# Low parts of weights and left multiplies of an attention stage on VectorE instead of GpSimd

## The chip, the cores and the metric

The kernel runs on one core of one Trainium2 chip. The core has TensorE (PE) for matmuls and transposes, VectorE (DVE) and ScalarE (ACT) for elementwise work, GpSimd (POOL) for elementwise work on SBUF, and SyncE (SP), which issues DMAs. The metric is the device time of one execution in microseconds, the median of several runs.

## The reference

One layer of a hybrid encoder: 1024 tokens, 1024 channels, float32. A normalised input is projected once; the parts feed a convolution branch and an attention branch, which are gated, merged and projected; then comes a SwiGLU block. The attention is a stick-breaking one with 8 heads of 64 channels. What is computed of a block of 128 queries:

```python
z = jnp.einsum('bqhd,bkhd->bhqk', qb, kb) * scale
log_1m = jnp.where(mask, jax.nn.log_sigmoid(-z), 0.0)
rev_excl = lax.cumsum(log_1m, axis=3, reverse=True) - log_1m
a = jnp.where(mask, jnp.exp(jax.nn.log_sigmoid(z) + rev_excl), 0.0)
outs.append(jnp.einsum('bhqk,bkhd->bqhd', a, vb))
```

So a weight is sigmoid(z) times the product of sigmoid(-z) over all later allowed keys.

## The kernel before

**Precision.** Matmul operands are kept as a high part and a low part; the low part is the operand less its high part. `load_w` (L64) does this for weights: a DMA of 128 x 1024 into `wraw`, an ACT copy into `wh` (L70), a subtraction into `wl` (L71). L71 runs on the engine given by `sub`, else on GpSimd. `mm3` and `dense_T` (L74 to L91) multiply with them; `wl` is read in the last third of a product (L80). Without an argument the tiles `wraw`, `wh` and `wl` have two buffers each.

**First stage, up to about 50 us.** Eight blocks of 128 tokens are fetched (`xt`), squared on ACT with the sum kept (`junk`, L172), scaled: DVE adds epsilon (`pv`, L101), GpSimd takes the power -1/2 (`pr`, L105), DVE multiplies (`xt`, L175). TensorE transposes (`tp`, L113), ACT and DVE make high and low parts (`hH` L115, `hL` L116), and a product for the values of heads 0 to 3 follows (`psv`, L137 to L139; `vt`, L142 and L143). The two weights of that product have `sub=V` already.

**Attention stage, about 50 to 352 us.** For each head and each pair of query blocks (m = 0 to 3), `chunk` makes a row of up to 512 keys: two matmuls into `z`, a mask on the diagonal (DVE, L246), sigmoid(-z) into one of two tiles `qf` (ACT, L251), sigmoid(z) into `sg` (L252). DVE then runs the product from right to left along the row (`R`: L255 for the chunk with the diagonal, L260 for the chunk left of it, which starts from the first one's last value) and multiplies by `sg` (L257, or L261 for the left chunk). L261 runs on GpSimd: 128 x 512, 32 times, only for m = 2 and 3 and thus for four rows of a head. GpSimd also writes a column of zeros into `R` (L256) and zeros into the unused quarter of `aH` and `aL` (L324). TensorE transposes the rows (`tpa`, L315), ACT and DVE split them (`aH` L320, `aL` L321), and TensorE multiplies with the values (`av`, L290 and L291), of which there is one PSUM buffer; ACT and DVE empty it (`avt` L296, `ar` L299).

**Work laid between.** A table (`at`) gives the projections of later heads and of the convolution branch to steps of this loop: `psk`, `psq`, `psv`, `psg`, each a product of 24 matmuls of 512 columns (or of 256 for `psv`). Fifteen weights are loaded for them from the first stage on: eight for keys and queries, two for values, five for the other branch.

**Order.** A scheduler sets the order on each engine from the program's order, its buffers and its own costs of the instructions; each engine then runs its list strictly in order.

Of the kernel before, what the change touches and what calls it, by code (L numbers as in the profile page):

```python
# [7 lines left out]
F32 = mybir.dt.float32  # L8
# [3 lines left out]
ALU = mybir.AluOpType  # L12
# [25 lines left out]
def layer_kernel(ctx, tc, x, vecs, dww, gains, ident_d, mask_d, wv, wi, wbr, wo, wu, wdq, wd, out):  # L38
    nc = tc.nc
    PE, V, A, G, SP = nc.tensor, nc.vector, nc.scalar, nc.gpsimd, nc.sync  # L40

    def pool(name, bufs=1, **kw):
        return tc.tile_pool(name=name, bufs=bufs, reuse_waits="tile", **kw)
# [17 lines left out]
    hH = big.tile([P, NK, S], F32R, name="hH")  # L61
    hL = big.tile([P, NK, S], F32R, name="hL")

    def load_w(src, pl=None, bufs=2, n=1024, sub=None):  # L64
        pl = pl or wst
        raw = wst.tile([P, 1024], F32, name="wraw", tag="wraw", bufs=2)[:, 0:n]
        SP.dma_start(out=raw, in_=src)
        wh = pl.tile([P, n], F32R, name="wh", tag="wh", bufs=bufs)
        wl = pl.tile([P, n], F32R, name="wl", tag="wl", bufs=bufs)
        A.activation(out=wh, in_=raw, func=AF.Copy)  # L70
        (sub or G).tensor_tensor(out=wl, in0=raw, in1=wh.bitcast(F32), op=ALU.subtract)  # L71
        return wh, wl

    def mm3(ps, steps, first=True, last=True):  # L74
# [72 lines left out]
    with pool("prep") as pp:  # L147
# [31 lines left out]
        fetch(1)  # L179
        transpose_split(psz, "z", xts[0], 0)  # L180
        wvt.append(load_w(wv[0, 0], pp, sub=V))
        pre(1)
        wvt.append(load_w(wv[0, 1], pp, sub=V))
        for tb in range(1, NT):
            if tb + 1 < NT:
# [49 lines left out]
    def chunk(par, qk, i, c, n, diag, carry):  # L235
        ks, (qhs, ql) = qk
        kst, qh = ks[par], qhs[par]
        r = slice(par * 64, par * 64 + 64)
        ts_ = slice(i * P, (i + 1) * P)
        nn = max(n, 256)  # L240
        z = psz.tile([P, HALF], F32, name="z", tag="z")
        cs = slice(c * HALF, c * HALF + nn)
        PE.matmul(z[:, 0:nn], lhsT=qh[:, ts_], rhs=kst[:, cs], start=True, stop=False)
        PE.matmul(z[:, 0:nn], lhsT=ql[par][:, ts_], rhs=kst[:, cs], start=False, stop=True)
        if diag:
            V.tensor_tensor(out=z[:, n - P:n], in0=z[:, n - P:n], in1=mask, op=ALU.add)  # L246
        sg = ap_.tile([P, HALF], F32, name="sg", tag="sg", bufs=3)
        q = qfix[qturn[0] % len(qfix)]
        qturn[0] += 1
        R = ap_.tile([P, HALF + 8], F32, name="R", tag="R", bufs=RBUFS)  # L250
        A.activation(out=q[:, 0:n], in_=z[:, 0:n], func=AF.Sigmoid, scale=-1.0)  # L251
        A.activation(out=sg[:, 0:n], in_=z[:, 0:n], func=AF.Sigmoid)  # L252
        if diag:
            d = q[:, 0:n][:, ::-1]
            V.tensor_tensor_scan(out=R[:, 3:3 + n][:, ::-1], data0=d, data1=d, initial=1.0, op0=ALU.mult, op1=ALU.bypass)  # L255
            G.memset(R[:, 3 + n:4 + n], 0.0)  # L256
            V.tensor_tensor(out=R[:, 4:3 + n], in0=sg[:, 0:n - 1], in1=R[:, 4:3 + n], op=ALU.mult)  # L257
        else:
            d = q[:, 1:n + 1][:, ::-1]
            V.tensor_tensor_scan(out=R[:, 4:4 + n][:, ::-1], data0=d, data1=d, initial=carry, op0=ALU.mult, op1=ALU.bypass)  # L260
            G.tensor_tensor(out=R[:, 4:4 + n], in0=sg[:, 0:n], in1=R[:, 4:4 + n], op=ALU.mult)  # L261
        return R

    def rows_of(h, m, qk):
        rows = []
        for ii in range(2):
            i = 2 * m + ii
            n_all = (i + 1) * P
            if n_all > HALF:
                r1 = chunk(h % 2, qk, i, 1, n_all - HALF, True, None)  # L270
                r0 = chunk(h % 2, qk, i, 0, HALF, False, r1[:, 3:4])
                rows.append((r0, r1))
            else:
                rows.append((chunk(h % 2, qk, i, 0, n_all, True, None), None))
        return rows
# [61 lines left out]
    def load_pair(pr, what):  # L337
        wts[what] = load_w(wi[(12 if what == "k" else 8) + pr])
        if what == "k":
            pairs[pr] = ([ap_.tile([P, S], F32R, name="kst", tag=f"k{j}", bufs=1 + j) for j in range(2)], None)  # L340
        else:
            qh = [ap_.tile([P, S], F32R, name="qh", tag=f"q{j}", bufs=1 + j) for j in range(2)]
            ql = [ap_.tile([P, S], F32R, name="ql", tag=f"ql{j}", bufs=1 + j) for j in range(2)]
            for j in range(2):
                G.memset(ql[j][64 - j * 64:128 - j * 64, :].bitcast(F32), 0.0)
            pairs[pr] = (pairs[pr][0], (qh, ql))
# [82 lines left out]
    def bank(nm):  # L429
        return ps8.tile([P, HALF], F32, name=nm, tag="d")  # L430

    with pool("mix") as mp:
        ones = mp.tile([P, P], F32, name="ones")
        avg = mp.tile([P, P], F32, name="avg")
# [641 lines left out]
    PE, V, A, G, SP = [Ordered(e) for e in (PE, V, A, G, SP)]  # L1076
# [152 lines left out]
```

## Time and profile before

| | |
|---|---|
| median of 3 runs (lowest, highest) | 1464.91 us (1461.34, 1465.78) |
| profiled execution | 1465.04 us |
| its span in the trace | 1463.2 us |
| busy: PE, DVE, ACT, POOL | 1374.1, 1057.3, 528.6, 282.3 us |
| low parts of weights on POOL (L71), whole program | 58 times, 141.0 us |
| left multiplies on POOL (L261) | 32 times, 46.7 us |

Busy time is that in which an engine executes an instruction; idle time ahead of an instruction is put down to what ended last before it. TensorE's busy time is modelled, since its instructions overlap. The granted clock is given as a share of 2.4 GHz. The chain of waits goes back from the last instruction: at each step to what released it, or to the one before it on its engine.

### The profile page before, as it was taken

The page shows a single profiled execution, that of the slowest core. Times are in us where ns is not written, and L with a number is a line of the kernel's source. Part 1 is how long each engine was busy: PE and PEld are TensorE (multiplying, and loading weights), DVE is VectorE, ACT ScalarE, POOL GpSimd, SP SyncE. Part 2 cuts the span into 40 slices and gives each one's busy share as a digit, 9 for nine tenths or more (in the row PEclk, how much of TensorE's full clock was granted, in tenths as well). Part 3 has the DMA queues.
Part 4 walks back from the last instruction along what each step waited for, and adds up shares of the span by engine and source line. Part 5 has one row for each costly group of instructions (what it writes and reads, how often), then busy time and mean ns, then how long its engine had stood idle before and what let it go on. Part 6 is the DMA issues. An engine that isn't in the chain of part 4 may idle for free.

```text
span 1463.2 us, 17209 instructions
## 1 busy us (share of the span) xinstructions
PE 1374.1 (94%) x6412; PEld 1126.8 (77%) x6412; DVE 1057.3 (72%) x1385; ACT 528.6 (36%) x863; POOL 282.3 (19%) x301
## 2 busy tenths in 40 slices
PE   6988998998999979999999799999999998999987
PEld 6866787777888757887787588888888887888875
DVE  5498878776999996325348899888877785644564
ACT  5466656553111104323325223222222222633450
POOL 2134323332324232322306200000000000000130
PEclk9999999999999989999999899999999999999999
DMA  6001001101111110212522155444444445965273
GB/s 221 23 26 40 22 23 32 42 30 36 45 49 52 43 44 22 65 43 81 172 87 94 65 198 184 174 157 158 143 149 162 166 137 178 371 230 177 89 272 100
DMA packets 62403, 160.97 MB, mean 110 GB/s; under 512 B 6384, under 2 KB 17904, under 8 KB 62320
## 3 DMA queue, kind: packets, MB, share of 16 engines
q1 hardware_dynamic: 62032, 158.83, 32.2%
q8 instruction: 50, 0.82, 0.2%
q10 hardware_dynamic: 288, 1.05, 0.2%
q14 instruction: 33, 0.27, 0.1%
HBM read 117.65 MB, written 40.11 MB: 108 GB/s over the span
## 4 chain that ended last, share of the span: by engine, by line
PE 66%; DVE 22%; issue 5%; ACT 3%; DMA 2%; POOL 2%; SPq 0%; DVEq 0%; POOLq 0%; ACTq 0%
PE m L914 28%; PE md L914 12%; DVE acc L453 11%; PE pg L77 2%; PE pg L78 2%; PE pg L80 2%; DVE R L260 2%; DVE R L255 2%; PE po L670 1%; PE po L669 1%; PE po L668 1%; DVE aL L321 1%; DVE R L257 1%; PE av L291 1%; PE pb L78 1%
## 5 line engine op out<-in xcount | busy, mean ns | idle before, releaser
L71 POOL TENSOR_TENSOR wl<-wraw,wh 128x1024 fp32r<-128x1024 f32 (+1 forms) x58 | 141.0, 2438 | 248.7 <-ACT wh L70 145.7
L453 DVE SCALAR_TENSOR_TENSOR acc<-u,dw,acc 128x1024 f32<-128x1024 f32 x120 | 176.9, 1531 | 0.3
L914 PE MATMUL m<-t,wh 128*128 128x512 f32 x528 | 134.8, 397 | 4.4 <-ACT wh L914 3.0
L914 PE MATMUL m<-hH,wh 128*128 128x512 f32 x328 | 130.6, 398 | 8.8 <-ACT wh L776 8.8
L914 PE MATMUL md<-wl,wh 128*128 128x512 f32 x308 | 122.5, 398 | 9.5 <-DVE wl L914 9.5
L914 PE MATMUL m<-hL,wh 128*128 128x512 f32 x328 | 129.9, 396 | 0.0
L914 PEld LDWEIGHTS m<-t,wh 128*128 128x128 f32 x528 | 100.0, 190 | 29.0 <-ACT wh L914 3.4
L914 PE MATMUL md<-wh 128*128 128x512 f32 x308 | 122.0, 396 | 0.0
L914 ACT ACTIVATE c<-c 128x512 f32<-128x512 f32 x44 | 27.8, 633 | 244.4 <-DVE c L914 244.4
L914 POOL TENSOR_TENSOR dc<-dc,gpo 128x512 f32<-128x512 f32 x4 | 5.1, 1301 | 541.4 <-ACT junk L914 541.4
L70 ACT ACTIVATE wh<-wraw 128x1024 fp32r<-128x1024 f32 (+1 forms) x60 | 56.5, 945 | 144.4 <-PE pg L78 50.7
L77 PE MATMUL pg<-hH,wh 128*128 128x512 f32 x256 | 101.5, 396 | 0.0
L78 PE MATMUL pg<-hL,wh 128*128 128x512 f32 x256 | 100.0, 391 | 0.0
L914 PE MATMUL md<-wh,wl 128*128 128x512 f32 x308 | 98.8, 395 | 0.0
L914 PE MATMUL m<-hH,wl 128*128 128x512 f32 x328 | 89.2, 393 | 0.0
L914 PEld LDWEIGHTS m<-hH,wh 128*128 128x128 f32 x328 | 62.2, 190 | 23.7 <-ACT wh L776 9.2
L914 PEld LDWEIGHTS md<-wl,wh 128*128 128x128 f32 x308 | 58.9, 191 | 24.5 <-DVE wl L914 11.8
L914 DVE TENSOR_TENSOR wl<-ra,wh 128x1024 fp32r<-128x1024 f32 (+1 forms) x42 | 48.4, 1153 | 38.1 <-ACT wh L914 38.0
L914 PEld LDWEIGHTS m<-hL,wh 128*128 128x128 f32 x328 | 62.2, 190 | 14.1
L914 PEld LDWEIGHTS m<-hH,wl 128*128 128x128 f32 x328 | 61.6, 188 | 14.3
L914 PE MATMUL m<-t,wl 128*128 128x512 f32 x264 | 70.7, 390 | 0.0
L914 DVE TENSOR_TENSOR u<-m,u 128x512 f32<-128x512 f32 x66 | 45.4, 688 | 33.5 <-PE m L914 32.1
(226 smaller groups left out, 3303.2 us busy)
## 6 DMA issues: line engine op xcount, KB each, us to landing
ra<-act SPq DMA_DIRECT2D x35, 512.0 KB, 6.8
wraw<-in_wi SPq DMA_DIRECT2D x32, 512.0 KB, 3.5
rg<-in_wu SPq DMA_DIRECT2D x23, 512.0 KB, 4.4
ru<-in_wu SPq DMA_DIRECT2D x22, 512.0 KB, 5.3
q<-in_wdq SPq DMA_DIRECT2D x22, 512.0 KB, 6.1
wsum<-q SPq DMA_DIRECT2D x22, 512.0 KB, 2.6
act<-sa SPq DMA_DIRECT2D x44, 256.0 KB, 2.7
rb<-wsum SPq DMA_DIRECT2D x20, 512.0 KB, 8.7
```

What stands on the lines that cost most here:

```text
L70: A.activation(out=wh, in_=raw, func=AF.Copy)
L71: (sub or G).tensor_tensor(out=wl, in0=raw, in1=wh.bitcast(F32), op=ALU.subtract)
L77: PE.matmul(ps, lhsT=lh, rhs=rh, start=(first and j == 0), stop=False)
L78: PE.matmul(ps, lhsT=lh, rhs=rl, start=False, stop=False)
L80: PE.matmul(ps, lhsT=ll, rhs=rh, start=False, stop=(last and j == n - 1))
L255: V.tensor_tensor_scan(out=R[:, 3:3 + n][:, ::-1], data0=d, data1=d, initial=1.0, op0=ALU.mult, op1=ALU.bypass)
L257: V.tensor_tensor(out=R[:, 4:3 + n], in0=sg[:, 0:n - 1], in1=R[:, 4:3 + n], op=ALU.mult)
L260: V.tensor_tensor_scan(out=R[:, 4:4 + n][:, ::-1], data0=d, data1=d, initial=carry, op0=ALU.mult, op1=ALU.bypass)
L291: PE.matmul(av, lhsT=vt[j][:, hh, :], rhs=aL[:, jj, :], start=False, stop=(j == 2 * m + 1))
L321: V.tensor_tensor(out=flat[1][:, 0:n * P], in0=tpf, in1=flat[0][:, 0:n * P].bitcast(F32), op=ALU.subtract)
L453: V.scalar_tensor_tensor(out=acc, in0=u[:, kk:kk + S], scalar=dw[:, cb, kk:kk + 1], in1=acc, op0=ALU.mult, op1=ALU.add)
L914: return lambda *a, **k: tc.keep_in_program_order(fn(*a, **k))
```

## The change

A variable holds the engine of L71 where no `sub` is given: VectorE up to the end of the attention stage, GpSimd after it. The multiply of the left chunk becomes a VectorE instruction.

```diff
+    low_of = [V]
...
-        (sub or G).tensor_tensor(out=wl, in0=raw, in1=wh.bitcast(F32), op=ALU.subtract)
+        (sub or low_of[0]).tensor_tensor(out=wl, in0=raw, in1=wh.bitcast(F32), op=ALU.subtract)
...
-            G.tensor_tensor(out=R[:, 4:4 + n], in0=sg[:, 0:n], in1=R[:, 4:4 + n], op=ALU.mult)
+            V.tensor_tensor(out=R[:, 4:4 + n], in0=sg[:, 0:n], in1=R[:, 4:4 + n], op=ALU.mult)
...
+    low_of[0] = G
     with pool("mix") as mp:
```

15 subtractions and 32 multiplies pass from GpSimd's list to VectorE's; no instruction is added or removed. Lines after the first insertion are numbered 2 higher in the kernel after (L71 is L73, L261 is L263), and the scheduler sets a new order on every engine within the first 352 us.

GpSimd in the first stage, before (`pr` is the power of a block, `wl` a low part):

```order
L105 TENSOR_TENSOR pr_213<-pv_211,mhalf_77 128x1
L71 TENSOR_TENSOR wl_554<-wraw_551,wh_553 128x1024
L105 TENSOR_TENSOR pr_265<-pv_263,mhalf_77 128x1
L71 TENSOR_TENSOR wl_562<-wraw_559,wh_561 128x1024
L105 TENSOR_TENSOR pr_317<-pv_315,mhalf_77 128x1
```

After, the same place on VectorE, where the two low parts now stand (`xt_258` is the block that `pr_265` scales):

```order
L103 TENSOR_SCALAR pv_263<-sst_261 128x1
L73 TENSOR_TENSOR wl_554<-wraw_551,wh_553 128x1024
L145 TENSOR_TENSOR vt_255<-psv_230,vt_255 128x4x64
L177 SCALAR_TENSOR_TENSOR xt_258<-xt_258,pr_265,gpre_101 128x1024
L118 TENSOR_TENSOR hL_79<-tp_268,hH_78 128x4x128
L118 TENSOR_TENSOR hL_79<-tp_275,hH_78 128x4x128
L145 TENSOR_TENSOR vt_307<-psv_282,vt_307 128x4x64
L103 TENSOR_SCALAR pv_315<-sst_313 128x1
L73 TENSOR_TENSOR wl_562<-wraw_559,wh_561 128x1024
```

The powers follow each other on GpSimd with nothing between, and a low part stands ahead of the scaling on VectorE.

VectorE in head 2 for m = 2 and 3, before (rows of the table `R` by number; L260 is the product of a left chunk, L257 the multiply of a diagonal chunk):

```order
L260 SCALAR_TENSOR_TENSOR R_1436<-qf1_549,R_1426 128x512
L255 SCALAR_TENSOR_TENSOR R_1446<-qf0_547 128x256
L246 TENSOR_TENSOR z_1497<-z_1497,mask_74 128x128
L257 TENSOR_TENSOR R_1446<-sg_1445,R_1446 128x255
L260 SCALAR_TENSOR_TENSOR R_1456<-qf1_549,R_1446 128x512
L255 SCALAR_TENSOR_TENSOR R_1502<-qf0_547 128x384
```

After:

```order
L262 SCALAR_TENSOR_TENSOR R_1436<-qf1_549,R_1426 128x512
L257 SCALAR_TENSOR_TENSOR R_1446<-qf0_547 128x256
L263 TENSOR_TENSOR R_1436<-sg_1435,R_1436 128x512
L259 TENSOR_TENSOR R_1446<-sg_1445,R_1446 128x255
L262 SCALAR_TENSOR_TENSOR R_1456<-qf1_549,R_1446 128x512
L323 TENSOR_TENSOR aL_1488<-tpa_1483,aH_1487 128x384
L263 TENSOR_TENSOR R_1456<-sg_1455,R_1456 128x512
```

The left multiply (L263) stands one or two instructions behind its product.

TensorE in the same phase, m = 3, before (`psk` is a projection of later heads):

```order
L243 MATMUL z<-kst,qh 128x512
L244 MATMUL z<-kst,ql 128x512
L291 MATMUL av<-aL,vt 128x256
L77 MATMUL psk<-hH,wh 128x512
L315 MATMUL tpa<-ident,R 128x128 x2
L78 MATMUL psk<-hL,wh 128x512
L243 MATMUL z<-kst,qh 128x512
```

After:

```order
L245 MATMUL z<-kst,qh 128x512
L246 MATMUL z<-kst,ql 128x512
L80 MATMUL psk<-hL,wh 128x512
L79 MATMUL psk<-hH,wh 128x512
L80 MATMUL psk<-hL,wh 128x512
L79 MATMUL psk<-hH,wh 128x512
L80 MATMUL psk<-hL,wh 128x512
L79 MATMUL psk<-hH,wh 128x512
L80 MATMUL psk<-hL,wh 128x512
L82 MATMUL psk<-hH,wl 128x512
L317 MATMUL tpa<-ident,R 128x128
L245 MATMUL z<-kst,qh 128x512
```

More of the projection stands ahead of the transposes of the left chunks. Counted up to the last `z` of a head, 3, 15, 14, 9 and 10 more matmuls of projections have been issued in heads 0, 1, 2, 3 and 5 than before; at the next query pair or two the counts are level again.

## Rows read from the trace of the kernel before

**Rows 1.** Chain of waits, 20 to 352 us: shares of the stretch by engine and line.
```profile
by line: DVE R L260 8.1%; issue 6.9%; DVE R L255 6.9%; DVE aL L321 5.3%; DVE R L257 4.5%; PE av L291 4.4%; PE tpa L315 4.2%; PE av L290 3.9%; PE psg L80 3.8%; PE psv L137 3.5%; PE psv L139 3.5%; PE psv L138 3.5%; PE psg L78 3.4%; PE psg L77
```

**Rows 2.** Windows of the attention stage: from:to and length, then the columns named.
```profile
core 0: us, PE busy (x) PEld busy (x) DVE busy (x) ACT busy (x) POOL busy (x), PEclk, DMA share, GB/s
20.00:352.00 332.00, 303.08 (x1786) 256.48 (x1786) 249.77 (x408) 185.56 (x377) 110.51 (x196) 0.99 0.13 37
20.00:40.00 20.00, 17.41 (x138) 17.11 (x138) 15.21 (x23) 13.02 (x25) 7.60 (x9) 0.91 0.51 159
76.00:121.00 45.00, 36.57 (x205) 28.52 (x204) 43.20 (x70) 29.11 (x64) 16.86 (x32) 1.00 0.08 21
121.00:139.00 18.00, 17.86 (x105) 14.50 (x103) 13.56 (x28) 11.44 (x24) 5.91 (x12) 1.00 0.24 63
139.00:152.00 13.00, 8.18 (x43) 6.17 (x42) 13.00 (x17) 7.95 (x18) 7.18 (x7) 1.00 0.05 17
152.00:170.00 18.00, 18.00 (x98) 15.75 (x97) 14.25 (x29) 10.28 (x22) 1.83 (x13) 0.91 0.06 15
245.00:261.00 16.00, 12.58 (x65) 9.72 (x64) 14.19 (x19) 8.53 (x17) 6.05 (x8) 1.00 0.07 17
261.00:280.00 19.00, 18.87 (x104) 15.52 (x104) 14.09 (x29) 11.51 (x24) 5.94 (x13) 1.00 0.19 51
```

**Rows 3.** Groups by line and shape, 20 to 352 us: busy us, mean ns | idle, releasers.
```profile
L71 POOL TENSOR_TENSOR wl<-wraw,wh 128x1024 fp32r<-128x1024 f32 x16 | 39.5, 2470 | 70.9 <-ACT wh L70 67.8 <-ACT sg L252 3.0
L261 POOL TENSOR_TENSOR R<-sg,R 128x512 f32<-128x512 f32 x32 | 46.7, 1461 | 81.1 <-DVE R L260 77.6 <-PE tpa L315 1.8 <-ACT aH L320 1.6
L257 DVE TENSOR_TENSOR R<-sg,R 128x511 f32<-128x511 f32 x16 | 14.9, 933 | 0.6
L257 DVE TENSOR_TENSOR R<-sg,R 128x255 f32<-128x255 f32 x16 | 13.4, 840 | 0.9
L255 DVE TENSOR_TENSOR_SCAN R<-qf 128x512 f32<-128x512 f32 x16 | 21.7, 1358 | 2.6 <-ACT qf L251 2.0 <-PE tpa L315 0.5
L175 DVE SCALAR_TENSOR_TENSOR xt<-xt,pr,gpre 128x1024 f32<-128x1024 f32 x5 | 8.5, 1703 | 3.8 <-POOL pr L105 3.8
```

**Rows 4.** Timeline of VectorE, two heads: start us, length us, instruction, count.
```profile
148.34 1.53 DVE L257 TENSOR_TENSOR R<-sg,R 128x511 f32<-128x511 f32 x1
...
152.23 1.20 DVE L321 TENSOR_TENSOR aL<-tpa,aH 128x512 fp32r<-128x512 f32 x2
...
157.02 0.41 DVE L257 TENSOR_TENSOR R<-sg,R 128x255 f32<-128x255 f32 x1
...
161.98 1.22 DVE L255 TENSOR_TENSOR_SCAN R<-qf 128x512 f32<-128x512 f32 x1
163.31 0.69 DVE L257 TENSOR_TENSOR R<-sg,R 128x511 f32<-128x511 f32 x1
```

**Rows 5.** Timeline of GpSimd beside the first row of group 4.
```profile
147.26 2.07 POOL L261 TENSOR_TENSOR R<-sg,R 128x512 f32<-128x512 f32 x1 [0.58 <-DVE R L260]
```

**Rows 6.** Timeline of VectorE while the input is normalised.
```profile
12.66 1.22 DVE L71 TENSOR_TENSOR wl<-wraw,wh 128x1024 fp32r<-128x1024 f32 x1
...
21.59 1.28 DVE L175 SCALAR_TENSOR_TENSOR xt<-xt,pr,gpre 128x1024 f32<-128x1024 f32 x1 [0.66 <-POOL pr L105]
...
23.99 0.14 DVE L101 TENSOR_SCALAR pv<-sst 128x1 f32<-128x1 f32 x1
...
26.38 3.38 DVE L175 SCALAR_TENSOR_TENSOR xt<-xt,pr,gpre 128x1024 f32<-128x1024 f32 x1 [0.99 <-POOL pr L105]
```

**Rows 7.** Timeline of GpSimd in the same stretch.
```profile
23.45 2.40 POOL L71 TENSOR_TENSOR wl<-wraw,wh 128x1024 fp32r<-128x1024 f32 x1 [1.90 <-ACT wh L70]
25.80 0.55 POOL L105 TENSOR_TENSOR pr<-pv,mhalf 128x1 f32<-128x1 f32 x1
```

**Rows 8.** Timeline of TensorE: transposes of the input, and eight matmuls of a projection.
```profile
29.91 1.94 PE L113 MATMUL tp<-ident,xt 128*128 128x128 f32 x8 [2.59 <-DVE xt L175]
...
58.23 1.98 PE L80 MATMUL psq<-hH,wl 128*128 128x512 f32 x8
```

## The prediction

> **What bounds the kernel now.** Everything that the change touches ends before 352 us, so I read that part alone. First the chain of waits [rows 1]: its longest single entries are VectorE's products, multiplies and low parts (L260, L255, L321, L257: 24.8% of the stretch), and the rest is TensorE's lines, each of 3 to 4%. GpSimd stands nowhere among them. So two engines take turns as the bound. The windows say where [rows 2]. Over 20 to 352 us TensorE is busy 303.1 us of 332 and VectorE 249.8; what TensorE can still gain here is its 28.9 us of idle time. From 139 to 152 us VectorE is busy all 13.0 us and TensorE 8.2: this is head 2 at m = 2 and 3, where the left chunks are. 76 to 121 us (heads 0 and 1: 43.2 us of 45) and 245 to 261 us (head 5: 14.2 of 16) look alike. Between them, at 121 to 139, 152 to 170 and 261 to 280 us, projections run, TensorE is full and VectorE has 4.4, 3.8 and 4.9 us free.
>
> Then the two engines beside each other. A multiply of 511 columns on VectorE took 0.69 us at 163.31, with GpSimd doing nothing, and 1.53 us at 148.34 [rows 4], while GpSimd's left multiply ran from 147.26 to 149.33, 2.07 us against a mean of 1.46 [rows 3, 5]. The two do not overlap; they wait for each other. The part of VectorE's busy time that is really such waiting is the key to this change.
>
> **The change part by part.** The sum is made against the profiled execution, 1465.04 us, which lies 0.13 us above the median of the three runs; its span is 1463.2 us, and the 1.8 us around it stay.
>
> *What VectorE gets.* A left multiply has 512 columns, as the low part `aL` at 152.23 us, of which two took 1.20 us [rows 4]: 0.60 us each in a row of work, 0.69 alone. 32 x 0.60 = 19.2 us. A low part of a weight took VectorE 1.22 us [rows 6], of which about 0.08 lies under the next instruction: 15 x 1.14 = 17.1 us. Together 36.3 us.
>
> *What VectorE no longer waits for.* From the means of groups 3 less the lengths alone: 255 columns (0.84 - 0.41) x 16 = 6.9; 511 columns (0.93 - 0.69) x 16 = 3.9; products of 512 columns (1.36 - 1.22) x 16 = 2.2; scaling of the input (1.70 - 1.28) x 5 = 2.1 [rows 3, 4, 6]. Together 15.1 us, and the net load is +21.2 us. Where it falls decides.
>
> *The saturated stretches* hold the left multiplies of heads 0, 1, 2 and 5. At 139 to 152 us three multiplies were delayed as the one in group 4, by 0.84 us each: 2.5 us given back against 4 x 0.60 = 2.4 added, net nothing. On the mean over the eight heads 10.8 / 8 = 1.35 us is given back (from the 255 and 511 columns), net +1.05 us per head. Four heads: between 0 and +4.2 us; I take +2.0.
>
> *The first stage.* GpSimd made a low part from 23.45 to 25.85 us, and the power of the next block, asked for by `pv` at 24.0, came only at 25.80 [rows 6, 7]. The scaling of that block then took 3.38 us instead of 1.28, and TensorE sat 2.59 us before its transposes at 29.91 [rows 6, 8]. The clock granted from 20 to 40 us is 0.91, between the two levels of 1.2 and 2.4 GHz, which is 1.8 us lost; the fall comes with this gap, and the eight transposes after it took 1.94 us. Without the low part on GpSimd the power is ready near 24.7. VectorE has the low part (1.14) and a `vt` ahead of the scaling, which then ends near 27.0 instead of 29.8, when TensorE runs out of earlier work at 27.3 (29.91 less 2.59). So the gap goes, and most of the lost clock: -2.6 - 1.4 = -4.0 us; between -1.5 (another wait takes half the gap, the clock still falls) and -4.4. TensorE has work from here to 76 us, so what is gained here stays.
>
> *The order on TensorE.* 15, 14 and 10 projection matmuls are issued earlier, inside the saturated phases of heads 1, 2 and 5, where TensorE is idle. One takes 0.25 us (eight in 1.98 [rows 8]): 3.7, 3.5 and 2.5 us, which the full stretches behind would lose. They can lose only what VectorE has free there, less two low parts of 1.14 in the first and the last: 2.1, 3.8 and 2.6 us [rows 2]. The smaller of each pair: 2.1 + 3.5 + 2.5 = 8.1 us at most. At least 0: TensorE also takes its list strictly in order, and a projection that stands before a `z` can hold back VectorE's next row. I take half, -4.0 us.
>
> *Elsewhere* (other weights, heads 3, 4, 6, 7) TensorE is the bound and VectorE's free time covers the load; I take 0. If the cover is gone it costs: the heads have 16 left multiplies at most, net 4 x 1.05 = 4.2 us, and a low part on the path 1.14 us. GpSimd is left with small fills, so the zeros that TensorE sometimes waits for come no later.
>
> Sum: 1465.0 - 4.0 + 2.0 - 4.0 = **1459 us**.
>
> **The rivals.** *The new order gives nothing (1463 us).* VectorE, 21 us heavier, needs all of its free time, and the projections moved forward only change which gap TensorE has: -4.0 + 2.0 alone. For it speaks that the full stretches had 13.1 us free on VectorE and four low parts and later splits go there; against it, that the moved matmuls lie exactly in the saturated phases.
>
> *VectorE becomes the bound (1472 us, slower).* Its list is strictly in order, and a low part waits for ACT's `wh`. On GpSimd this wait was long, 67.8 us over the stage [rows 3], and cost nothing, since only small fills stood behind. On VectorE the products, multiplies and splits of the next row stand behind, and for those ACT, TensorE's transposes and the one `av` buffer wait. If half of the net load ends on the path: -4.0 + 10.6 = +6.6; all of it would be 1482. It decides as soon as the low parts stand ahead of their `wh`, or VectorE's free time in a projection stretch is less than the two low parts put there (2.3 us of 4.4 at 121 to 139 us). The Trainium skill, "Perfetto Trace Analysis", section "Optimizing Scalar/DVE Operations", speaks for this rival: with a saturated VectorE it may make sense to give work away, to GpSimd too, and this change does the reverse. The same section adds that the two share a read port of SBUF, so that moving between them might not help; the rows of group 4 and 5 agree with that second half, 1.53 us against 0.69.
>
> *All idle time in the saturated phases is used (1452 us).* The moved matmuls give all 8.1 us, and the saturated heads cost 0 instead of 2, with a little off TensorE's waits for the left rows: 1465.0 - 4.4 - 8.1 = 1452.5. For it: GpSimd's multiply ended some 1.3 to 2 us behind its product, VectorE's 0.7.
>
> That the change doesn't do what it says is excluded by the order: 47 instructions stand on the other engine.
>
> **How the numbers follow.** A measurement of this kernel can tell about 0.3%, 4.4 us, from no change. Forecast 1459 (itself 1455 to 1462): 0.42, of which 0.34 lies more than 4.4 us below the time before. New order gives nothing: 0.26, no change. VectorE the bound: 0.22, of which 0.18 is slower by more than 4.4 us. All idle time used: 0.10. Faster 0.34 + 0.10 = 0.44; slower 0.18; within 0.3% 0.38. The range reaches from 1450, the last rival with a little more off the first stage's waits, to 1470, the first part of the slower one.
>
> **What would show it.** Right: the multiplies of 255 and 511 columns at 0.41 and 0.69 us throughout; a left multiply of 0.69 us on VectorE; no gap of 2.6 us on TensorE near 30 us and a granted clock near 1.0 there; the conv stage starting about 6 us earlier than 352 us with its own length unchanged; VectorE still full in head 2, TensorE's idle time of 28.9 us down by some 6. Wrong: idle time on VectorE in front of low parts, ended by ACT's `wh`; TensorE's waits for `ar` and `aL` grown; the first stage ending as late as before; or a loss of clock in a place that had none.

## The result, and the profile after

| | before | after |
|---|---|---|
| median (lowest to highest, runs) | 1464.64 us (1461.34 to 1465.78, 4) | 1452.53 us (1452.17 to 1453.70, 4) |
| ratio, 95% interval | | 0.9922 (0.9905 to 0.9940) |
| profiled execution's span | 1463.2 us | 1450.4 us |

The changed kernel is faster by 0.8%, 12.1 us by the medians. By the traces 10.8 of 12.8 us lie in the attention stage: its end (the first low part of the attention outputs) moves from 353.1 to 342.3 us, and what follows takes nearly as long as before (1110.1 us before, 1108.1 after). The line numbers after are those of before plus 2 (plus 3 behind the attention stage).

The same windows as in [rows 2], for the changed kernel. The first is the stage; the others are the ramp, heads 0 and 1, the stretch behind them, head 2 at m = 2 and 3, the stretch behind it, and head 5:

```profile
core 0: us, PE busy (x) PEld busy (x) DVE busy (x) ACT busy (x) POOL busy (x), PEclk, DMA share, GB/s
20.00:341.00 321.00, 302.97 (x1777) 252.75 (x1775) 266.08 (x453) 183.12 (x376) 31.39 (x149) 0.99 0.13 38
20.00:40.00 20.00, 19.57 (x168) 19.23 (x166) 17.37 (x28) 13.95 (x27) 6.33 (x11) 1.00 0.51 164
72.00:116.00 44.00, 39.41 (x213) 30.45 (x213) 42.47 (x74) 29.00 (x63) 4.30 (x23) 1.00 0.05 16
116.00:133.00 17.00, 16.44 (x102) 13.42 (x100) 16.64 (x33) 11.89 (x27) 1.35 (x11) 1.00 0.17 48
133.00:147.00 14.00, 12.28 (x57) 8.34 (x55) 13.56 (x22) 7.36 (x15) 1.36 (x4) 1.00 0.14 39
147.00:163.00 16.00, 15.71 (x90) 12.83 (x91) 15.46 (x31) 10.86 (x25) 1.37 (x11) 1.00 0.07 16
236.00:252.00 16.00, 13.59 (x60) 10.44 (x59) 15.25 (x23) 9.22 (x17) 0.59 (x5) 0.89 0.07 17
```

TensorE is as busy as before (303.0 us against 303.1), in 321 us instead of 332: its idle time fell from 28.9 to 18.0 us, and that is the gain. VectorE's busy time rose from 249.8 to 266.1 us. In the saturated places TensorE's idle time fell from 8.4 us of 45 to 4.6 of 44 (heads 0 and 1), from 4.8 of 13 to 1.7 of 14 (head 2), from 3.4 of 16 to 2.4 of 16 (head 5). VectorE is still full in head 2, 13.6 us of 14, and these places are about as long as before: what changed is that TensorE does more in them.

What TensorE waited for in the stage; each row gives the waiting line, the releaser, us in total, times and the longest. First the kernel before:

```profile
PE av L290 <- DVE ar L299: 7.8, 5, 1.8
PE tpa L315 <- DVE aL L321: 7.4, 4, 2.2
PE av L291 <- DVE aL L321: 3.5, 6, 1.4
PE tpa L315 <- POOL R L256: 3.1, 2, 1.7
PE tpa L315 <- POOL R L261: 2.7, 2, 1.4
PE tp L113 <- DVE xt L175: 2.6, 1, 2.6
```

Then the changed kernel:

```profile
PE tpa L317 <- DVE aL L323: 5.1, 5, 1.9
PE av L293 <- DVE aL L323: 5.0, 8, 1.3
PE av L292 <- DVE ar L301: 2.2, 3, 1.2
PE tpa L317 <- DVE R L259: 1.4, 3, 0.6
PE tpa L317 <- DVE R L263: 1.3, 3, 0.6
```

The waits for GpSimd's `R` (3.1 + 2.7 us, one line being its multiply, the other a fill queued behind it) are gone, and 2.7 us of waits for VectorE's `R` took their place. The waits for `ar` fell from 7.8 to 2.2 us, the one for `xt` from 2.6 to 0.4. Those for `aL` stayed: 10.9 before, 10.1 after. Together -11.7 us, against -10.9 us of idle time: smaller waits grew by 0.8 us, above all those of `z` for ACT's `sg`, from 0.2 to 1.2.

The groups by line and shape on VectorE (busy us, mean ns, then idle time just before and its releasers), which answer to [rows 3]:

```profile
L263 DVE TENSOR_TENSOR R<-sg,R 128x512 f32<-128x512 f32 x32 | 21.7, 680 | 1.2 <-DVE R L262 0.5
L257 DVE TENSOR_TENSOR_SCAN R<-qf 128x512 f32<-128x512 f32 x16 | 19.4, 1213 | 0.7 <-ACT qf L253 0.7
L73 DVE TENSOR_TENSOR wl<-wraw,wh 128x1024 fp32r<-128x1024 f32 x15 | 18.3, 1217 | 8.4 <-PE psg L82 5.8 <-ACT wh L72 1.7 <-PE psq L82 0.8
...
L259 DVE TENSOR_TENSOR R<-sg,R 128x511 f32<-128x511 f32 x16 | 10.9, 682 | 0.4
...
L259 DVE TENSOR_TENSOR R<-sg,R 128x255 f32<-128x255 f32 x16 | 6.7, 420 | 0.2
L177 DVE SCALAR_TENSOR_TENSOR xt<-xt,pr,gpre 128x1024 f32<-128x1024 f32 x5 | 6.4, 1283 | 1.2 <-POOL pr L107 1.1
```

Every form now has the length that it had alone. The 255 columns went from 840 to 420 ns on the mean, the 511 from 933 to 682, the scaling of the input from 1703 to 1283. For what follows I call **hold-up** the net time by which VectorE's instructions with a GpSimd instruction of over 0.25 us beside them are longer than the median of the same form and line without one, summed over the attention stage from 20 us on (some are a little shorter and count against it). It is 17.7 us in the kernel before and 0.0 after; 22 instructions are clearly longer, by over 0.05 us each, and these are counted in brackets below.

### The profile page after: what moved, and what is told of

It reads as the page before. It is cut to its first block, busy times and chain, and to the rows that moved or that the text cites. A ratio compares the mean times of both kernels' runs of the same rounds, so it can differ in the third digit from the quotient of the medians.

```text
span 1450.4 us, 17204 instructions
## 1 busy us (share of the span) xinstructions
PE 1371.0 (95%) x6412; PEld 1120.5 (77%) x6412; DVE 1073.4 (74%) x1432; ACT 527.8 (36%) x863; POOL 203.6 (14%) x254
## 4 chain that ended last, share of the span: by engine, by line
PE 64%; DVE 23%; issue 5%; ACT 3%; POOL 2%; DMA 2%; SPq 0%; DVEq 0%; POOLq 0%; ACTq 0%
PE m L917 28%; PE md L917 12%; DVE acc L456 11%; PE pg L79 2%; PE pg L82 2%; PE pg L80 2%; DVE R L262 2%; DVE R L257 2%; PE po L673 1%; PE po L672 1%; DVE aL L323 1%; PE po L671 1%; DVE R L259 1%; PE tpa L317 1%; PE psg L82 1%
## 5 line engine op out<-in xcount | busy, mean ns | idle before, releaser
L456 DVE SCALAR_TENSOR_TENSOR acc<-u,dw,acc 128x1024 f32<-128x1024 f32 x120 | 177.0, 1534 | 0.3
L73 POOL TENSOR_TENSOR wl<-wraw,wh 128x1024 fp32r<-128x1024 f32 (+1 forms) x43 | 104.3, 2434 | 192.2 <-PE pg L82 96.7
```

Of the source, the lines that this page charges most:

```text
L73: (sub or low_of[0]).tensor_tensor(out=wl, in0=raw, in1=wh.bitcast(F32), op=ALU.subtract)
L456: V.scalar_tensor_tensor(out=acc, in0=u[:, kk:kk + S], scalar=dw[:, cb, kk:kk + 1], in1=acc, op0=ALU.mult, op1=ALU.add)
```

## The experiments

Two theories stood against each other. The prediction's own: separate gains (a shorter first stage, projections moved ahead on TensorE) against a heavier VectorE; they should add up. The other: while any two-input work stays on GpSimd, it and VectorE hold each other up, and what counts is that both kinds of work leave. In the first four expectations the prediction's account is theory 1 and the hold-ups are theory 2; in the later ones the hold-ups are theory 1. The kernels were timed in four groups, each beside the kernel before, whose median was 1464.6, 1464.9, 1465.3 and 1466.0 us in them. "us" is (ratio - 1) x 1465, and a difference of two such numbers is uncertain by about 2 to 3 us. Differences between kernels are given by the ratios, with that of the medians in brackets.

| kernel | median us | ratio (95% interval) | us | hold-up us (instructions) |
|---|---|---|---|---|
| changed kernel | 1452.53 | 0.9922 (0.9905 to 0.9940) | -11.4 | 0.0 |
| low parts alone moved | 1460.98 | 0.9972 (0.9961 to 0.9983) | -4.1 | 10.0 (14) |
| multiplies alone moved | 1468.41 | 1.0021 (1.0012 to 1.0030) | +3.1 | 12.8 (10) |
| first two low parts alone | 1462.44 | 0.9986 (0.9978 to 0.9995) | -2.1 | 15.6 (21) |
| all but the first two low parts | 1456.21 | 0.9939 (0.9927 to 0.9951) | -8.9 | 2.0 (1) |
| spare work on GpSimd, free to run ahead | 1472.95 | 1.0050 (1.0035 to 1.0064) | +7.3 | 2.0 (8) |
| spare work on VectorE, free to run ahead | 1457.32 | 0.9944 (0.9929 to 0.9960) | -8.2 | 0.0 |
| left multiplies of heads 0, 1, 2, 5 on GpSimd | 1460.71 | 0.9966 (0.9953 to 0.9978) | -5.0 | 6.8 (10) |
| left multiplies of heads 3, 4, 6, 7 on GpSimd | 1454.68 | 0.9929 (0.9913 to 0.9945) | -10.4 | 3.2 (4) |
| spare work on GpSimd behind each left multiply | 1458.00 | 0.9952 (0.9936 to 0.9968) | -7.0 | 4.8 (18) |
| multiplies alone, low parts in quarters | 1460.46 | 0.9965 (0.9954 to 0.9976) | -5.1 | 5.0 (15) |
| low parts of `load_w` on VectorE in the whole program | 1448.65 | 0.9887 (0.9869 to 0.9905) | -16.6 | 0.0 |

**The two halves of the change.** The low parts alone:

```diff
-            V.tensor_tensor(out=R[:, 4:4 + n], in0=sg[:, 0:n], in1=R[:, 4:4 + n], op=ALU.mult)
+            G.tensor_tensor(out=R[:, 4:4 + n], in0=sg[:, 0:n], in1=R[:, 4:4 + n], op=ALU.mult)
```

> Only the 15 low parts of weights go to VectorE; the 32 left multiplies stay on GpSimd. The order on TensorE now has 2, 3 and 1 projection matmuls moved ahead in heads 2, 3 and 5 up to the last z, where the changed kernel has 14, 9 and 10. Theory 1 (the order fills TensorE's idle time in the saturated phases): the first stage's 4.6 us and nothing more, 1460 us; the products' multiplies of 255 and 511 columns still take about 0.8 and 0.9 us in the mean. Theory 2 (what counts is only that GpSimd no longer holds VectorE up): the first stage's 4.6 us, less the 13 other low parts, 14.8 us of VectorE time against 4.8 us given back, half of the difference on the path: 1465 us. If low parts on VectorE cover all of the gain: 1453 us.

And the multiplies alone:

```diff
-        (sub or low_of[0]).tensor_tensor(out=wl, in0=raw, in1=wh.bitcast(F32), op=ALU.subtract)
+        (sub or G).tensor_tensor(out=wl, in0=raw, in1=wh.bitcast(F32), op=ALU.subtract)
```

> Only the 32 left multiplies go to VectorE; low parts stay on GpSimd. The first stage is that of the kernel before. Up to the last z, 15, 4 and 6 projection matmuls are moved ahead in heads 1, 2 and 5 (changed kernel 15, 14, 10). Theory 1 (order): about half of the gain behind the first stage, 1464.6 - 4 = 1461 us. Theory 2 (port): the multiplies give VectorE back 10.7 us for 19.2 added, so no gain, 1465 to 1468 us. If the multiplies carry all of the 6 us behind the first stage: 1458 us.

One half gains 4.1 us, the other loses 3.1, both with intervals that exclude 0: the sum is -1.0, and both together give -11.4. The effects don't add up. The order on TensorE is a part of that at most: in heads 1, 2 and 5 the halves move 3 and 25 projection matmuls ahead and the whole change 39, and the 11 that are more come to 2.8 us (0.25 us each [rows 8]) of the 10.4. With the multiplies alone GpSimd keeps its longest work. One of its low parts there, in GpSimd's timeline (start, length, instruction, idle time before):

```profile
130.37 2.63 POOL L71 TENSOR_TENSOR wl<-wraw,wh 128x1024 fp32r<-128x1024 f32 x1 [2.56 <-ACT wh L70]
```

VectorE's timeline beside it:

```profile
129.18 0.55 DVE L257 TENSOR_TENSOR R<-sg,R 128x383 f32<-128x383 f32 x1
129.65 1.22 DVE L255 TENSOR_TENSOR_SCAN R<-qf 128x512 f32<-128x512 f32 x1
130.97 2.58 DVE L257 TENSOR_TENSOR R<-sg,R 128x511 f32<-128x511 f32 x1
133.47 0.68 DVE L233 SCALAR_TENSOR_TENSOR ql<-psq,qh 64x512 fp32r<-64x512 f32 x1
```

TensorE's timeline:

```profile
133.61 0.55 PE L315 MATMUL tpa<-ident,R 128*128 128x128 f32 x3 [2.46 <-DVE R L257]
```

The multiply of 511 columns, 0.69 us alone [rows 4], took 2.58 us, from its start until about 0.5 us behind the end of GpSimd's low part. TensorE's transposes of that row waited 2.46 us for it. There are fewer held instructions than before the change (10 instead of 22), but they are the long ones. The page "SBUF — State Buffer" of the Trainium skill, section "SBUF: two separate sides", says that a VectorE instruction with two SBUF inputs and a GpSimd instruction that reads SBUF contend for an exclusive lock, held for the whole instruction; these rows agree.

**Is it the length of GpSimd's instruction?** The same kernel, with each low part on GpSimd in four pieces, and the same order of the projections on TensorE:

```diff
-        (sub or G).tensor_tensor(out=wl, in0=raw, in1=wh.bitcast(F32), op=ALU.subtract)
+        c = 1 if sub else cuts[0]
+        for j in range(c):
+            x = slice(j * (n // c), (j + 1) * (n // c))
+            (sub or G).tensor_tensor(out=wl[:, x], in0=raw[:, x], in1=wh.bitcast(F32)[:, x], op=ALU.subtract)
```

> As the run with the multiplies alone on VectorE (1468.4 us, 3.1 above the kernel before beside it), but in the attention stage each low part that GpSimd makes is cut into four instructions of 256 columns. The order on TensorE is the same as there. Theory 1 (a two-input instruction of VectorE is blocked until GpSimd's instruction ends): VectorE gets in between the quarters, no multiply of 511 columns is held for 2.3 us or more, the lengthening of 12.4 us in sum falls to 4 to 8, and the time falls by 3 to 6 us, to 1462 to 1465. Theory 2 (the loss there comes from VectorE's 19 us more of work): 1467 to 1470 us, since GpSimd only gets a little slower.

1460.5 us: 8.2 (8.0) us below the uncut version, somewhat more than expected. (The 12.4 us of the expectation are the hold-up by a rougher rule; the table has 12.8.) GpSimd's timeline at the same place in the program:

```profile
131.75 3.54 POOL L76 TENSOR_TENSOR wl<-wraw,wh 128x256 fp32r<-128x256 f32 x4 [2.58 <-ACT wh L72]
```

and VectorE's:

```profile
131.01 1.22 DVE L260 TENSOR_TENSOR_SCAN R<-qf 128x512 f32<-128x512 f32 x1
132.34 0.97 DVE L262 TENSOR_TENSOR R<-sg,R 128x511 f32<-128x511 f32 x1
133.23 0.67 DVE L238 SCALAR_TENSOR_TENSOR ql<-psq,qh 64x512 fp32r<-64x512 f32 x1
133.83 0.54 DVE L326 TENSOR_TENSOR aL<-tpa,aH 128x384 fp32r<-128x384 f32 x1
```

The multiply takes 0.97 us instead of 2.58. GpSimd's four pieces take 3.54 us instead of 2.63, so GpSimd pays and VectorE gets in between. The splits behind it (`ql`, `aL`), which read one of their inputs from PSUM, have their usual 0.67 and 0.54 us beside GpSimd's work. VectorE's 19 us of additional work are the same in both kernels, so they alone are not what made the uncut version slow.

**The price of work and the price of a hold-up.** Spare work that nobody reads, 64 multiplies of 192 columns, first on VectorE behind each left multiply:

```diff
+            spare = ap_.tile([P, 192], F32, name="spare", tag="spare", bufs=1)
+            V.tensor_tensor(out=spare, in0=hH[:, 0, 0:192].bitcast(F32), in1=hL[:, 0, 0:192].bitcast(F32), op=ALU.mult)
+            V.tensor_tensor(out=spare, in0=hH[:, 0, 0:192].bitcast(F32), in1=hL[:, 0, 0:192].bitcast(F32), op=ALU.mult)
```

> The changed kernel, and behind each left multiply VectorE makes the two unused multiplies of 192 columns, 64 in all, an estimated 0.25 to 0.30 us each by the 0.60 us of a multiply of 512: 16 to 19 us more on VectorE. If VectorE's free time covers load in this stage (what the prediction's term 'elsewhere 0' and theory 1 say), the time rises by no more than 4 us, to 1456 us. If VectorE is what bounds the stage, most of it is paid: 1462 to 1471 us.

Then the same two lines on GpSimd:

> The changed kernel, and behind each left multiply GpSimd makes two multiplies of 192 columns whose output nobody reads (inputs hH and hL, which stand still in this stage). The order of the projections on TensorE is that of the changed kernel, VectorE's work is the same, and nobody waits for the spare work. Theory 1 (the gain beyond the first stage comes from GpSimd's two-input work no longer holding up VectorE's): VectorE's instructions between 45 and 345 us are lengthened by 6 to 12 us in sum, as in the kernel before, the granted clock or TensorE's idle time there gets worse, and the time is 1456 to 1461 us. Theory 2 (the gain comes from the handover of R and from the order of the projections): 1452 to 1454 us, since both are as in the changed kernel.

The load on VectorE cost 3.2 (4.8) us. From 20 us to the end of the stage VectorE is busy 286.1 us, against 266.8 in the changed kernel: about 0.2 us for each of 19.3. Every instruction kept its length. But this is the price of work in VectorE's free time, not in its full stretches. The inputs stand still, so 43 of the 64 multiplies run before the first left multiply, 30 of them between 40 and 60 us, where VectorE of the changed kernel is busy 4.7 us of 20; and the order on TensorE is another too. What work costs in the full stretches was not measured.

The run on GpSimd did not test what it was meant to either. The spare multiplies were queued ahead of the rows they belonged to and ran in one block up to 91 us, and a fill that TensorE's transposes need stood behind them. GpSimd's timeline at the block's end:

```profile
90.41 0.59 POOL L266 TENSOR_TENSOR spare<-hH,hL 128x192 f32<-128x192 f32 x1
90.93 0.13 POOL L258 MEMSET R<- 128x1 f32 x2
```

TensorE's waits from 60 to 120 us (in total, times, longest):

```profile
PE tpa L320 <- POOL R L258: 16.1, 2, 11.0
```

Two waits of 11.0 and 5.1 us, and the kernel is 18.7 (20.4) us slower than the changed one. It shows how much hangs on GpSimd's small fills, since its list is in order too: the prediction's remark that they "come no later" was a condition, not a detail. So the spare work was tied to its row, by inputs that are ready only then:

```diff
+            spare = ap_.tile([P, 192], F32, name="spare", tag="spare", bufs=1)
+            G.tensor_tensor(out=spare, in0=sg[:, 0:192], in1=R[:, 4:196], op=ALU.mult)
+            G.tensor_tensor(out=spare, in0=sg[:, 192:384], in1=R[:, 196:388], op=ALU.mult)
```

> The changed kernel, and behind each left multiply GpSimd makes two multiplies of 192 columns that read sg and the finished R and whose output nobody reads, so that they can't run ahead into the first heads as those of the earlier run did. VectorE's work and the order on TensorE are the changed kernel's; nobody waits for the spare work but the next owner of R and sg. Theory 1 (GpSimd's two-input work holds up VectorE's): lengthened VectorE instructions of 3 to 8 us in sum between 45 and 345 us, two thirds to all of which beside the left chunks of heads 0, 1, 2 and 5, and 1455 to 1459 us. Theory 2 (only the handover of R and the order count): 1452 to 1454 us.

VectorE's own work and the order on TensorE are those of the changed kernel, and nobody waits for GpSimd's output; only the buffers of `sg` and `R` come free later (one wait for them, 0.6 us). It costs 4.4 (5.5) us, with 4.8 us of hold-up. Two groups on VectorE, 45 to 345 us (columns as above):

```profile
L262 DVE TENSOR_TENSOR_SCAN R<-qf,R 128x512 f32<-128x512 f32 x32 | 44.3, 1386 | 0.0
...
L259 DVE TENSOR_TENSOR R<-sg,R 128x511 f32<-128x511 f32 x16 | 10.9, 682 | 0.4
```

and on GpSimd:

```profile
L266 POOL TENSOR_TENSOR spare<-sg,R 128x192 f32<-128x192 f32 x32 | 30.7, 961 | 2.2
L265 POOL TENSOR_TENSOR spare<-sg,R 128x192 f32<-128x192 f32 x32 | 26.7, 834 | 103.6 <-ACT sg L254 63.5 <-DVE R L263 37.2 <-ACT avt L301 2.5
```

The product of a left chunk has 1386 ns instead of the 1276 of the changed kernel, and GpSimd's multiplies 0.83 and 0.96 us instead of the 0.59 that they took alone above. So a us of hold-up cost 0.9 to 1.1 us, and in the run with the quarters (7.8 us less of it, 8.2 us gained) about as much. None of TensorE's larger waits ends on GpSimd here; those for `aL` are longer, 13.0 us against 10.1.

**Where the multiplies count.** `rows_of` sets the engine of the left multiply by head; in the first kernel heads 0, 1, 2 and 5 go back to GpSimd, in the second the others:

```diff
     def rows_of(h, m, qk):
         rows = []
+        mul_of[0] = G if h in (0, 1, 2, 5) else V
```

> The changed kernel, but the left multiplies of heads 0, 1, 2 and 5 (the stretches in which VectorE is full) stand on GpSimd again, 16 of 32. All 32 of them cost 8.5 us (low parts alone moved against the changed kernel). If the gain belongs to the full stretches: 1458 to 1461 us. If it is spread evenly: 1456 to 1457 us. If it belongs to heads 3, 4, 6 and 7: 1452 to 1454 us.

> The changed kernel, but the left multiplies of heads 3, 4, 6 and 7 stand on GpSimd again, 16 of 32. If the gain of 8.5 us belongs to the full stretches of heads 0, 1, 2 and 5: 1452 to 1454 us; if it is spread evenly 1456 to 1457; if it belongs to these heads 1458 to 1461. With the run before it: whether the two halves add up to 8.5 us.

The saturated heads cost 6.4 (8.2) us, the others 1.0 (2.2); the sum, 7.4 (10.3), is near what all 32 cost (11.4 - 4.1 = 7.3; 8.5). So four fifths or more of what the multiplies gain belongs to the full stretches. In the second kernel none of TensorE's larger waits ends on GpSimd. In the first they are back; TensorE's waits, 20 to 351 us:

```profile
PE tpa L319 <- DVE aL L325: 7.9, 5, 2.5
...
PE tpa L319 <- POOL R L259: 3.0, 2, 1.6
...
PE tpa L319 <- POOL R L264: 2.3, 3, 1.3
```

5.3 us of handover and 6.8 of hold-up come back together, and the new order on TensorE goes: at the last `z` of heads 1, 2 and 5, 0, 2 and 3 projection matmuls are moved ahead instead of 15, 14 and 10. The shares of the three in the 6.4 us were not separated. In the second kernel most of the order stays (15, 14 and 7).

**The first stage.** The low parts of the first two weights alone, on top of the kernel before:

```diff
-        wts[what] = load_w(wi[(12 if what == "k" else 8) + pr])
+        wts[what] = load_w(wi[(12 if what == "k" else 8) + pr], sub=V if pr == 0 else None)
```

> The kernel before, with only the low parts of the first two projection weights (those made while the input is normalised) on VectorE. TensorE's order is that of before but for one transpose. Both theories: the scaling that took 3.38 us takes 1.28, TensorE's gap of 2.59 us before the transposes near 30 us goes, and with it the fall of the clock: 1464.6 - 4.6 = 1460 us. If VectorE's own low part takes the place of the gap: 1463 us or more.

And the changed kernel with these two on GpSimd:

> The changed kernel, with the low parts of the first two projection weights left on GpSimd. TensorE's order is that of the changed kernel but for one transpose. If the gains add up, it lacks just what the kernel with only those two gains: 1452.5 + 4.6 = 1457 us. If the saturated phases absorb a later start (VectorE has work left that waits for nothing of the first stage), it lacks less: 1453 to 1455 us.

In the trace the first projection of the heads starts 3.0 us earlier (46.2 us instead of 49.1), but the stage ends only 0.6 us earlier: half of the gain is gone at the last `z` of head 2 (1.5 us left), nearly all at that of head 4 (0.4). The hold-ups are still there; that they take it is not shown. The measured 2.1 us (interval 0.7 to 3.2) are more than the trace of the stage accounts for, and that difference stays open. Taken out of the changed kernel the same two low parts cost 2.5 (3.7) us: there the stage ends 2.3 us later, and the gain of the first stage stays to the end.

This last kernel lacks the first stage's gain, so beside the kernel before it shows what the rest of the change does. TensorE's timeline at the last `z` of heads 2 and 4, first in the kernel before:

```profile
143.85 0.40 PE L244 MATMUL z<-kst,ql 128*128 128x512 f32 x1
...
213.87 0.39 PE L244 MATMUL z<-kst,ql 128*128 128x512 f32 x1
```

then in the changed kernel with the two low parts on GpSimd:

```profile
143.84 0.40 PE L246 MATMUL z<-kst,ql 128*128 128x512 f32 x1
...
208.83 0.39 PE L246 MATMUL z<-kst,ql 128*128 128x512 f32 x1
```

In head 2 the `z` comes at the same time, but TensorE has 14 more projection matmuls behind it, 3.5 us of work. In head 4, where the counts are level again, it comes 5.0 us earlier. So up to there the full stretches got no shorter; TensorE got more done in them. The last `z` of head 4 in three more kernels with level counts, each from TensorE's timeline: with the left multiplies of heads 0, 1, 2 and 5 on GpSimd, with the spare work behind each left multiply, and the changed kernel:

```profile
213.62 0.40 PE L247 MATMUL z<-kst,ql 128*128 128x512 f32 x1
...
209.82 0.40 PE L246 MATMUL z<-kst,ql 128*128 128x512 f32 x1
...
205.63 0.40 PE L246 MATMUL z<-kst,ql 128*128 128x512 f32 x1
```

The second and the third have the same order and differ by the spare work and its hold-ups, 4.2 us. The first lacks the new order and has hold-ups, 3.8 us behind the second; those two also differ in VectorE's load and in the waits for GpSimd's `R`, so that this is a reading of what the order brings and no test of it.

**What remains on GpSimd.** The changed kernel gives the low parts back to GpSimd behind the attention stage. Without that line:

```diff
-    low_of[0] = G
```

> The changed kernel without the line that gives the low parts behind the attention stage back to GpSimd: those of the conv and mixing stages (21 more, 58 us on GpSimd) stand on VectorE too. There, between 343 and 548 us, the 120 multiply-adds of the convolution take 1.53 us on the mean and 1.28 us when GpSimd does nothing. Theory 1: the 31 us of lengthening go, 21 x 1.14 = 24 us are added, and VectorE's sum there falls by some 7 us; if VectorE bounds the conv stage the time is 1444 to 1450 us, if TensorE does, 1451 to 1454. Against it: in this stage low parts in VectorE's list wait for ACT's high parts, and the taps behind them with them: 1455 to 1465 us.

1448.65 us, the fastest kernel of this study: 5.1 (3.9) us below the changed one. The line moves 43 low parts, more than the 21 of the expectation; six that other lines make later stay on GpSimd. But the place is not the expected one. In the conv stage the 120 multiply-adds went from a mean of 1534 ns to 1306, 27 us of VectorE time, against 23 us of low parts that came, and the stage took 226 us instead of 224: what was held up there was not on the path (TensorE is busy 209.3 us of the 224). The gain comes behind it. TensorE's waits from 560 to 780 us in the changed kernel:

```profile
PE po L673 <- POOL wl L73: 3.6, 3, 1.7
PE po L671 <- ACT wh L72: 0.8, 2, 0.6
```

and with all low parts on VectorE:

```profile
PE tp L726 <- DVE xr L711: 0.2, 1, 0.2
```

Where the output projection `po` starts, TensorE waited 3.6 us for GpSimd's low parts (2.4 us each) and 0.8 for the high parts; with low parts of 1.2 us on VectorE these 4.4 us are gone.

## Why the prediction was right or wrong

The forecast was 1459 us, the result 1452.5: inside the range of 1450 to 1470, faster as the largest chance had it, but twice the forecast gain. The 1452 us of the last rival are met, and in part by its mechanism: TensorE's idle time in the saturated places fell by 7.9 us, near the 8.1 that it gave to the moved matmuls. That these alone bring it is not shown.

- **The first stage (-4.0): right in place, near in size.** The first projection of the heads starts at 44.55 us instead of 49.13, -4.6; with the two low parts on GpSimd it starts at 47.69, so 3.1 us are theirs. The window from 20 to 40 us has a clock of 1.00 (0.91 before) and TensorE busy 19.6 us (17.4). The reading "what is gained here stays" holds in the changed kernel and not by itself: with the two low parts alone moved, the stage gave it back.
- **What VectorE gets and no longer waits for: near.** All hold-ups went, as assumed. They were 17.7 us and not 15.1, mainly since the multiplies of 383 columns and the products of 384 were left out; in busy time it was +16.3 us instead of +21.2.
- **The saturated stretches (+2.0, 0 to +4.2) and the order on TensorE (-4.0): here the sum was mis-sized.** Together they were put at -2.0 us. Taking the 16 multiplies there back, and the order with them, costs 6.4 us (8.2 by the medians). The trade on VectorE was even up to the last `z` of head 2, as the lower end of the range had it, and cost 0.8 us in head 5. What TensorE does meanwhile was taken at half: 14 and 10 matmuls in heads 2 and 5 are 6.0 us, an estimate from 0.25 us each, and gains of that kind follow behind these heads, 5.0 us up to head 4 and 2.9 from head 5 to head 6; the 15 in head 1 show none by the last `z` of head 2. What the sum lacked is that a held multiply or product stands on TensorE's path at once (2.46 us of wait for a multiply held to 2.58) and that GpSimd's `R` came later than VectorE's; a us given back was set against a us of work.
- **Elsewhere (0): too cautious.** TensorE's waits for `ar` fell from 7.8 to 2.2 us; with the low parts alone moved they are 2.3, and with the first two alone they are as before, so it is the low parts behind these that bring this; by which way the runs don't show. The multiplies of heads 3, 4, 6 and 7 add 1.0 us. The prediction had counted both only as a load that is covered.
- **The order by itself: not shown.** With the multiplies alone on VectorE, 15, 4 and 6 projection matmuls are moved ahead in heads 1, 2 and 5, and that kernel is slower than before; the spare work behind the left multiply keeps the whole new order and loses 4.4 us. The order is thus not enough. What it is worth alone was not tried: it follows from which engine the instructions stand on, and no run sets it alone.
- **VectorE becomes the bound (1472): its sign was there, its price not.** With the low parts alone moved VectorE stood idle 15.7 us before them, 11.2 of it behind ACT's `wh`, and the kernel was still 4.1 us faster; in the changed kernel it is 8.4 us, 1.7 by `wh`. The Trainium skill's "Perfetto Trace Analysis", section "Optimizing Scalar/DVE Operations", which the prediction named for this rival, says that giving work from a saturated VectorE to GpSimd may make sense and warns that the shared port may spoil it; here the warning decided, and more than "might not help": the share on GpSimd cost time.
- **A loss of clock in a place that had none** also came: 0.89 from 236 to 252 us, between the two levels of 1.2 and 2.4 GHz, where [rows 2] has 1.00 (2.4 GHz) for the same part of head 5; TensorE's longest wait in the stage, 1.9 us for `aL` at 247 us, lies in it. The 0.91 behind head 2 went in exchange (1.00 from 147 to 163 us).

What stays open: how the 6.4 us of the saturated heads divide into handover, hold-up and order, what the new order is worth alone, what a us of work costs in a full stretch, and 1.5 us of the first-two-parts run.

## What to carry to other kernels

Before weighing an engine's load in us, sort its busy time into work and waiting: compare each form's mean with its shortest instances, and see what runs on GpSimd beside the long ones. A us of hold-up cost about 1 us where the engines take turns as the bound (and little or nothing in the conv stage), a us of additional work in VectorE's free time about 0.2, so taking work back from GpSimd can pay although the engine that takes it is the fuller one. Look also at what the other engine does meanwhile: the full stretches got no shorter here, TensorE got more done in them. Move all of it or cut what stays into short pieces: one half of this change, the multiplies alone, made the kernel slower.

## What the runs showed of the hardware

- The hold goes both ways. In the changed kernel the power `pr` of 128 x 1 on GpSimd, 0.54 us alone, took 1.39 us while VectorE made a low part. GpSimd's timeline:

```profile
19.88 0.54 POOL L107 TENSOR_TENSOR pr<-pv,mhalf 128x1 f32<-128x1 f32 x1 [2.85 <-DVE pv L103]
23.15 1.39 POOL L107 TENSOR_TENSOR pr<-pv,mhalf 128x1 f32<-128x1 f32 x1 [2.72 <-DVE pv L103]
```

and VectorE's:

```profile
22.92 1.22 DVE L73 TENSOR_TENSOR wl<-wraw,wh 128x1024 fp32r<-128x1024 f32 x1
```

- Kernels with hold-ups seem to scatter more. Before the change, 29 runs on one chip lie between 1461.6 and 1467.8 us, 11 with the multiplies alone moved between 1465.5 and 1470.1; 4 of the changed kernel have 1452.2 to 1453.7, 6 with the spare work on VectorE 1456.5 to 1458.5. Fewer runs also spread less, so this is a hint; that the scatter comes from which of the two engines gets in first is only argued.
- A scan on VectorE with both data inputs in SBUF is held like a multiply: the product of 512 columns of a row's last chunk, 1213 ns on the mean in the changed kernel, had 1362 with the multiplies alone moved.
